# Queries, keys and values of a two-layer attention kernel: earlier requests, second buffers, merged transfers

## The chip, the cores and the metric

The kernel runs on one core of a Trainium2 chip. The metric is the device time of one execution in microseconds (us). Beside the plain runs there is one execution that was taken with the hardware profiler. All times of stages and instructions below come from that one.

## The reference

The program is a small diffusion backbone with two layers over 1024 latent tokens, with a prefix of 256 context tokens, width 1024, in fp32. The even layer (here "layer 0") has two groups of attention heads: A is global attention with 8 query heads on 2 key/value heads, and B is attention in a band of 128 tokens to either side, with a learned sink. The odd layer ("layer 1") has a convolution branch and attention D over a 2-D neighbourhood, 8 heads with a bias table. Cut to what matters here:

```python
def even_mixer(h_lat, h_ctx, w_in, w_out, ...):
    aq, ak, av, ag, bq, bk, bv, bg = project(h_lat)      # and the same of h_ctx
    aq, ak, bq, bk = (apply_rope(t, cos, sin) for t in (aq, ak, bq, bk))
    ka = concat([c_ak, ak], axis=1); va = concat([c_av, av], axis=1)
    oa = lax.map(lambda qb: gqa_attend(qb, ka, va), qa_blk)           # blocks of 128 queries
    ob = lax.map(b_block, (arange(n_blk), qb_blk))                    # context + band, bias, sink
    y = concat([oa * silu(ag), ob * silu(bg)], -1) @ w_out

def odd_mixer(...):
    oc = conformer_conv(cv, cgl, cg, ...)
    od = lax.map(d_row, (arange(rows), q_rows))   # softmax(q k^T * scale + bias) v, per head
    y = concat([oc, od * silu(dg)], -1) @ w_out

def reference(...):
    for i in range(2):
        h = rms_norm(x, norm_g[i]) * (1 + sc) + sh      # sc, sh, g = split(silu(c) @ mod_w[i] + mod_b[i])
        x = x + g * mixer(h)
    return rms_norm(x_lat, final_g)
```

## The kernel before

**Arithmetic.** Every fp32 operand of a large product is split into a high part (rounded) and a low part, and a product is three matmuls: high x high, high x low, low x high (`mm3`, L317 to L319; `split`, L297 and L300). In attention the scores need two matmuls of a tile (L444 and L448) because high and low parts of a 64-wide head lie above each other in 128 rows: `QH` holds the high part of the queries twice, `QL` the low part and some rows for the maximum; `KA` holds the high part of the keys in rows 0 to 63 and the low part in rows 64 to 127, and `KB` holds the high part once more.

**Way through DRAM.** Projections write queries, keys, values and gates to DRAM tensors (`Qd`, `Kd`, `Vd`, `Gs` in layer 0; `QD`, `KD`, `VD`, `GD` in layer 1), and the attention reads them back in another layout. In layer 0 `proj_qkv` makes them for a unit `u` (one key/value head with its four query heads), and `qk_tail` transposes one block of 128 tokens and writes its `Q` and `K` (L808, L809).

**Attention.** `attn_gen` walks over groups. In layer 0 a group is one block of 128 queries of a unit with 2, 4, 5 or 10 key tiles, ten groups for each of four units (order `ORDER`, `QORD`); in layer 1 a group is one head and one half of the latent tokens, with 7 tiles. For each tile it issues the two score matmuls into a bank `st`, the exponential on ScalarE (L456), the split into `ph` and `pl`, and three tiles later (`look`) the three products with the values into `ov` (L407 to L409). Before a group can begin, its preparation (`attn_prep`) has to be through: it requests `QH` and `QL` (`load_q`), multiplies queries and keys for the row maximum (`maxes`, banks `mx`: L548, L560, L568 in layer 0, L1245, L1253 in layer 1), and writes the maximum into rows of `QL` (L386). The preparation of group gi + 2 is a generator that is advanced while group gi runs: `g.step` steps for each tile, with what is left drained at the group's last tile. After the request it makes four empty steps before the first product.

**Buffers and loads.** In layer 0 `KA` has two buffers, `KB` and the values `V` one each. `load_ka` reads the whole of a unit's keys, in two halves, when the queries of its first group are requested; `load_kb` and the load of `V` follow when the first group begins. In layer 1 `load_head` reads the keys of the next head (L357, L358) and copies them to `KB` on ScalarE (L359); the queries come in three transfers (L1205 to L1207). All these are issued by the SyncE queue, in order. At the start the tiles of `mod_w` use the same buffers (`mw_tile`).

**Order.** `weave` interleaves the steps of `attn_gen` with filling work: the projections of the next unit (`fill0`), the output projections, in layer 1 `d_proj` and `out1_part`. A scheduler then orders the instructions of each engine by priority and by a modelled time. On the chip each engine runs its own list in order. Layer 0's attention runs from about 110 to 900 us, layer 1's from about 1110 to 1550 us.

The lines of the profile are lines of this kernel; the parts that the change touches:

Of the kernel before, what the change touches and what calls it, by code (L numbers as in the profile page):

```python
# [18 lines left out]
P = 128  # L19
# [12 lines left out]
BSO = (0, 256, 608, 1120, 1440)  # L32
BMO = (0, 320, 320, 760)
LOOK0, LOOK1 = 3, 3
AHEAD = 3
BMB = 2
CWB = 12
# [51 lines left out]
def tile_kernel(ctx: ExitStack, tc: tile.TileContext, a, out):  # L89
# [72 lines left out]
    @contextmanager  # L162
# [189 lines left out]
        GP.memset(KB[64:68, :].bitcast(F32), 1.0)  # L352
        Ks.append((KA, KB))

    def load_k(k, kh, kl):
        KA, KB = Ks[k % len(Ks)]
        SY.dma_start(KA[0:64, :].bitcast(F32), kh)  # L357
        SY.dma_start(KA[64:128, :].bitcast(F32), kl)  # L358
        SC.copy(KB[0:64, :], KA[0:64, :].bitcast(F32))  # L359

    def attn_prep(pool, g):
        QH = pool.tile([P, 512], F32R, tag="QH", name=nm("QH"), bufs=3)
        QL = pool.tile([P, 512], F32R, tag="QL", name=nm("QL"), bufs=3)
        g.QH, g.QL = QH, QL
        g.load_q(QH, QL)
        for _ in range(4):
            yield
        mp = pool.tile([P, 4, 4], F32, tag="mp", name=nm("mp"), bufs=2)
        if g.sink is not None:
            sk1, sk8 = g.sink  # L370
            SC.copy(mp[:, :, g.nmp], sk8)
# [12 lines left out]
        tr2 = bank("tr", nm("trn"))  # L384
        PE.transpose(tr2[0:nr, 0:P], nmt[:, 0:nr].bitcast(F32), ident)
        VE.tensor_tensor(QL[64 : 64 + nr, :].rearrange("p (h q) -> p h q", h=4),  # L386
                         tr2[0:nr, None, 0:P].broadcast_to([nr, 4, P]),
                         bd[0:nr, :, None].broadcast_to([nr, 4, P]), op=ALU.mult)

    def attn_gen(pool, groups, vshare, look, nexts=None):  # L390
# [30 lines left out]
                g.finish(g.ov, rb)  # L421

        for p in preps[:2]:
            for n_, _ in enumerate(p):
                if n_ % 2:
                    yield
        for gi, g in enumerate(groups):
            ids = [gi + 2] if gi + 2 < len(groups) else []
            if nexts is not None and gi in nexts:
                ids = nexts[gi]  # L430
            g.next = chain.from_iterable(preps[k] for k in ids)
            g.step = -(-18 * len(ids) // len(g.tiles))
        for g, t in items[:AHEAD]:
            g.ahead(t)
        for x, (g, t) in enumerate(items):
            if x + AHEAD < len(items):
                items[x + AHEAD][0].ahead(items[x + AHEAD][1])
            if t == 0:
                g.start()
            k, q0, n, extra = g.tiles[t]  # L440
            KA, KB = g.k()
            st = bank("st", nm("st"))
# [16 lines left out]
            pend.append((g, t, ph, pl))  # L459
            if t == len(g.tiles) // 2:  # L460
                g.gate()
            for _ in range(g.step // 2):
                next(g.next, None)
            yield
            if len(pend) > look:
                flush()
            for _ in range(g.step - g.step // 2):
                next(g.next, None)
            if t == len(g.tiles) - 1:
                for _ in g.next:  # L470
                    pass
            yield
        while pend:
            flush()
# [39 lines left out]
    KAs, KBs = [None] * 4, [None] * 4  # L514

    def load_ka(u):
        KAs[u] = a0.tile([P, NTOK], F32R, tag="KA", name=nm("KAt"), bufs=2)
        SY.dma_start(KAs[u][0:64, :].bitcast(F32), Kd[u][:, 0, :])
        SY.dma_start(KAs[u][64:128, :].bitcast(F32), Kd[u][:, 1, :])

    def load_kb(u):
        KB = KBs[0]
        SY.dma_start(KB[0:64, :].bitcast(F32), Kd[u][:, 0, :])

    def group0(u, qb):
        isb = u >= 2

        first = qb == QORD[0]
# [13 lines left out]
        def maxes(QH, mp):  # L542
# [12 lines left out]
            for hd in range(4):  # L555
# [7 lines left out]
                else:  # L563
# [30 lines left out]
        def finish(ov, rb):  # L594
# [9 lines left out]
            else:  # L604
# [5 lines left out]
        g = Group(load_q=load_q, start=(lambda: load_kb(u)) if first else (lambda: None), bias=False, ahead=lambda t: None, gate=gate, v=lambda k: Vs[0][:, k, :], load_v=(lambda: SY.dma_start(Vs[0][:, :, 0:128].bitcast(F32), Vd[u])) if first else None, maxes=maxes, nmp=1 if qb < 2 else (2 if isb else 3),  # L610
                  sink=(sink[:, hs : hs + 4], sink8[:, hs : hs + 4]) if isb else None, skm=lambda: sk, k=lambda: (KAs[u], KBs[0]),
                  tiles=[(k, 0, 512, x) for k, x in kt], den=den, finish=finish)
        g.prep = attn_prep(kvp, g)
        return g
# [4 lines left out]
    with ExitStack() as p0x:  # L619
# [181 lines left out]
        def qk_tail(u, j, pc):  # L801

            tr = bank("tr", nm("trk"))
            for i in range(3):
                PE.transpose(tr[:, i * P : (i + 1) * P], pc[:, i * P : (i + 1) * P], ident)
            qs = ap.tile([P, 2, 384], F32R, tag="qs", name=nm("qs"), bufs=2)
            split(tr[:, 0:384], qs[:, 0, :], qs[:, 1, :], "s", "v")
            SY.dma_start(Qd[u][j].rearrange("p a b t -> p a (b t)"), qs[:, :, 0:256].bitcast(F32))  # L808
            mark[0] = SY.dma_start(Kd[u][:, :, j * P : (j + 1) * P], qs[0:64, :, 256:384].bitcast(F32))  # L809

        def mod_steps():
            for part in (2,):
# [14 lines left out]

        def fill0(k, w=None):
            yield from proj_qkv(ORDER[k], w)
            yield from proj_gate(ORDER[k], gblocks(k)[0])  # L830

        for _ in fill0(0, w0):
# [1 line left out]
        solo[0] = False  # L834
        while hold[0]:
            next(mods)
        v_tiles(a0, 10)
        KBs[0] = a0.tile([P, NTOK], F32R, tag="KB", name="KBt")
        GP.memset(KBs[0][64:68, :].bitcast(F32), 1.0)
# [121 lines left out]
    with ExitStack() as l1x:  # L961
# [229 lines left out]
        v_tiles(dpool, 7, 2)  # L1191
        od = [None, None]

        def load_head(hd):
            i, e = divmod(hd, 2)
            ds = slice(e * 64, (e + 1) * 64)
            load_k(hd, KD[i][ds, 0, :], KD[i][ds, 1, :])

        def group1(gi, hd, hf):
            i, e = divmod(hd, 2)  # L1200
# [30 lines left out]
            def start():  # L1231
                if hf == 0 and hd < 7:
                    load_head(hd + 1)
                for j, k, n in ((0, 0, 2), (2, 2 + 5 * hf, 5)):
                    SY.dma_start(Vs[gi % 2][:, j : j + n, 0:128].bitcast(F32), VD[i][:, k : k + n, e])

            def maxes(QH, mp):
                KA = Ks[hd % len(Ks)][0]
# [27 lines left out]
            def finish(ov, rb):  # L1266
# [6 lines left out]
                if i == 3:  # L1273
# [1 line left out]
                    return  # L1275
                SY.dma_start(O1d[ds, i, hf], y[ds])

            g = Group(load_q=load_q, maxes=maxes, nmp=2, bias=True, ahead=ahead, sink=None, tiles=tiles, den=den, finish=finish,
                      start=start, gate=gate,
                      k=lambda: Ks[hd % len(Ks)], load_v=None, v=lambda k: Vs[gi % 2][:, k if k < 2 else k - 5 * hf, :])  # L1280
            g.prep = attn_prep(kvp, g)
            return g
# [1 line left out]
        SEQ = [(hd, hf) for hd in range(6) for hf in range(2)] + [(hd, hf) for hf in range(2) for hd in (6, 7)]  # L1284
        groups1 = [group1(gi, *x) for gi, x in enumerate(SEQ)]
        load_head(0)
        x2, ocs, od3, fin = [], [], [], [0]

        def out1_alloc():
# [246 lines left out]
```

## Time and profile before

| | |
|---|---|
| median of 3 runs | 1595.51 us (1594.14 to 1599.56) |
| the profiled execution | 1597.87 us |
| its span, first to last instruction | 1596.1 us |
| TensorE busy | 1466.4 us (92%) |
| VectorE / ScalarE / GpSimd busy | 1127.4 / 757.0 / 836.3 us |
| mean granted clock of TensorE | 0.96 |
| DMA, mean over the span | 139 GB/s, 222.01 MB |

The profile's page gives, for each engine, the time in which it was busy, then the span in 40 slices, the DMA queues, the chain of work that ended last, and the costliest groups of instructions. A group's line reads: source line, engine, operation, output <- inputs, shape, count, busy time, mean duration, and the idle time of the engine ahead of it with what ended it. PE is TensorE's matmul, PEld its weight load, DVE VectorE, ACT ScalarE, POOL GpSimd, SP SyncE; a "q" behind a name is that engine's issuing side. A matmul's own duration includes its way through the array; one of 512 columns starts 0.23 us after the one before it at full clock.

### The profile page before, as it was taken

The page shows a single profiled execution, that of the slowest core. Times are in us where ns is not written, and L with a number is a line of the kernel's source. Part 1 is how long each engine was busy: PE and PEld are TensorE (multiplying, and loading weights), DVE is VectorE, ACT ScalarE, POOL GpSimd, SP SyncE. Part 2 cuts the span into 40 slices and gives each one's busy share as a digit, 9 for nine tenths or more (in the row PEclk, how much of TensorE's full clock was granted, in tenths as well). Part 3 has the DMA queues.
Part 4 walks back from the last instruction along what each step waited for, and adds up shares of the span by engine and source line. Part 5 has one row for each costly group of instructions (what it writes and reads, how often), then busy time and mean ns, then how long its engine had stood idle before and what let it go on. Part 6 is the DMA issues. An engine that isn't in the chain of part 4 may idle for free.

```text
span 1596.1 us, 22238 instructions
## 1 busy us (share of the span) xinstructions
PE 1466.4 (92%) x6984; PEld 1185.4 (74%) x6984; DVE 1127.4 (71%) x2170; ACT 757.0 (47%) x1544; POOL 836.3 (52%) x762
## 2 busy tenths in 40 slices
PE   6889989998999989989999979999999899899895
PEld 1788867787788667668887658888777678778684
DVE  4898887488857677455568776999564466776676
ACT  2721343445444655655454664443342355545473
POOL 1561454455546667756455665665442344355575
PEclk9999989999999999999999999999999899999996
DMA  8548234532452123571111121212646778898732
GB/s 316 177 146 277 79 102 128 172 98 83 142 151 66 43 69 109 176 206 45 54 40 41 56 96 43 93 58 101 205 143 199 230 207 248 247 258 247 209 97 106
DMA packets 198654, 222.01 MB, mean 139 GB/s; under 512 B 19004, under 2 KB 154888, under 8 KB 198536
## 3 DMA queue, kind: packets, MB, share of 16 engines
q1 hardware_dynamic: 191872, 209.02, 42.9%
q10 hardware_dynamic: 6664, 11.57, 2.4%
q8 instruction: 55, 0.90, 0.2%
q14 instruction: 63, 0.52, 0.1%
HBM read 160.49 MB, written 60.03 MB: 138 GB/s over the span
## 4 chain that ended last, share of the span: by engine, by line
PE 64%; DVE 13%; DMA 12%; issue 4%; POOL 3%; ACT 2%; SPq 1%; DVEq 0%; POOLq 0%; ACTq 0%
PE p L317 6%; PE p L318 6%; PE p L319 6%; PE ov L409 4%; PE ov L407 4%; PE po L317 3%; PE ov L408 3%; PE po L318 3%; PE po L319 3%; PE st L448 3%; PE st L444 3%; PE pq L318 2%; PE pq L317 2%; PE pq L319 2%; PE pg L317 2%
## 5 line engine op out<-in xcount | busy, mean ns | idle before, releaser
L300 POOL TENSOR_TENSOR pl<-pf,ph 128x512 fp32r<-128x512 f32 (+4 forms) x321 | 394.1, 1239 | 283.4 <-ACT ph L297 226.3
L300 POOL TENSOR_TENSOR wl<-wr,wh 128x256 fp32r<-128x256 f32 (+2 forms) x256 | 199.6, 795 | 231.6 <-ACT wh L297 187.0
L456 ACT ACTIVATE pf<-st 128x512 f32<-128x512 f32 x284 | 166.3, 597 | 171.2 <-PE st L448 127.6
L297 ACT CAST ph<-pf 128x512 fp32r<-128x512 f32 (+4 forms) x364 | 209.1, 588 | 36.1 <-PE ov L408 20.8
L317 PE MATMUL p<-hh,wh 128*128 128x512 f32 x448 | 181.2, 406 | 6.1 <-DVE spq L1087 3.0
L297 ACT CAST wh<-wr 128x256 fp32r<-128x256 f32 (+2 forms) x264 | 102.7, 404 | 166.5 <-DMA wr<-in_ev_qkv_dram 40.7
L318 PE MATMUL p<-hl,wh 128*128 128x512 f32 x448 | 180.9, 405 | 0.0
L319 PE MATMUL p<-hh,wl 128*128 128x512 f32 x448 | 176.4, 402 | 0.0
L407 PE MATMUL ov<-ph,Vt 128*128 128x512 f32 (+4 forms) x364 | 142.5, 392 | 9.7 <-DVE y L598 6.4
L409 PE MATMUL ov<-pl,Vt 128*128 128x512 f32 (+4 forms) x364 | 142.9, 393 | 5.4 <-POOL pl L300 5.3
L444 PE MATMUL st<-QH,KAt 128*128 128x512 f32 (+4 forms) x364 | 141.9, 391 | 4.5 <-ACT pf L456 3.8
L408 PE MATMUL ov<-ph,Vt 128*64 128x512 f32 (+4 forms) x364 | 140.0, 385 | 0.0
L448 PE MATMUL st<-QL,KBt 68*128 68x512 f32 (+4 forms) x364 | 138.4, 389 | 0.7 <-DVE QL L386 0.7
L1027 DVE SCALAR_TENSOR_TENSOR cps<-U,taps,cps 128x512 f32<-128x512 f32 x184 | 125.2, 749 | 0.4
L561 DVE TENSOR_REDUCE mp<-mx 128x1 f32<-128x512 f32 x128 | 86.0, 683 | 48.9 <-PE mx L560 48.3
L220 DVE SCALAR_TENSOR_TENSOR macc<-mw,csil,macc 128x512 f32<-128x512 f32 x107 | 94.4, 902 | 21.6 <-DMA mw<-in_mod_w_dram 19.5
L317 PEld LDWEIGHTS p<-hh,wh 128*128 128x128 f32 x448 | 86.2, 192 | 29.1 <-issue 3.6
L319 PEld LDWEIGHTS p<-hh,wl 128*128 128x128 f32 x448 | 86.3, 193 | 20.8 <-issue 0.5
L318 PEld LDWEIGHTS p<-hl,wh 128*128 128x128 f32 x448 | 86.0, 192 | 18.9
L409 PEld LDWEIGHTS ov<-pl,Vt 128*128 128x128 f32 x364 | 70.5, 194 | 29.6 <-POOL pl L300 9.0
L407 PEld LDWEIGHTS ov<-ph,Vt 128*128 128x128 f32 x364 | 70.7, 194 | 26.1 <-issue 7.7
L319 PE MATMUL pq<-wh,hl 128*128 128x384 f32 x256 | 87.9, 345 | 0.7 <-DVE hl L311 0.7
(276 smaller groups left out, 3529.0 us busy)
## 6 DMA issues: line engine op xcount, KB each, us to landing
mw<-in_mod_w_dram SPq DMA_DIRECT2D x34, 512.0 KB, 5.5
Q<-qs SPq DMA_DIRECT2D x40, 256.0 KB, 2.7
QH<-Q SPq DMA_DIRECT2D x80, 128.0 KB, 2.8
wr<-in_od_d_dram SPq DMA_DIRECT2D x64, 128.0 KB, 2.6
mw<-in_mod_w_dram SPq DMA_DIRECT2D x28, 256.0 KB, 3.1
wr<-in_ev_qkv_dram SPq DMA_DIRECT2D x32, 192.0 KB, 3.6
KAt<-KD SPq DMA_DIRECT2D x16, 384.0 KB, 6.5
wr<-in_od_wo_dram SPq DMA_DIRECT2D x48, 128.0 KB, 3.2
```

The costliest lines, as they stand in the source:

```text
L297: SC.copy(hi, src)
L300: (GP if leng == "g" else VE).tensor_tensor(lo, src, hi.bitcast(F32), op=ALU.subtract)
L317: PE.matmul(o, lh, rh, start=first, stop=False)
L318: PE.matmul(o, lh, rl, start=False, stop=False)
L319: PE.matmul(o, ll, rh, start=False, stop=last)
L407: PE.matmul(o, V[:, 64:192], ph[:, :n], start=(t == 0), stop=False)
L408: PE.matmul(g.ov[0:64, q0 : q0 + n], V[:, 0:64], ph[:, :n], start=False, stop=False)
L409: PE.matmul(o, V[:, 64:192], pl[:, :n], start=False, stop=(last and g.sink is None))
L444: sts.append(PE.matmul(st[:, :n], KA[:, cs], g.QH[:, q0 : q0 + n], start=True, stop=False))
L448: PE.matmul(st[:, :n], KB[0:68, cs], g.QL[0:68, q0 : q0 + n], start=False, stop=True)
L456: SC.activation(pf[:, :n], st[:, :n], AF.Exp, scale=1.0 if g.bias else SCALE)
L1027: VE.scalar_tensor_tensor(pc, uc, w, pc, op0=ALU.mult, op1=ALU.add)
```

## The change

- Preparation in `attn_gen`: the request for the queries is issued when group gi begins (`next(preps[k])`), and the steps after it, the first products among them, may run from 3 tiles later on in layer 0 and 4 in layer 1 (`LEAD`). From then on `prepare` makes a fixed number of steps for each tile (`rate`: 2 or 3 for each open preparation) in place of `g.step` and the drain at the group's end.
- Layer 0's `KB` and `V` have two buffers (`kv_tiles`), so the `mod_w` tiles of the start have them too. Keys and values of the next unit are read in three pieces (`PIECES`: blocks 0 to 1, 2 to 5, 6 to 9), each as soon as its last block has been written by `qk_tail`. `KB` is filled by a copy on ScalarE (`copy_k`) in the last tile of the last group but one of the unit before; the first unit's is read from DRAM.
- Transfers: `Kd` is laid out as it is needed, high above low, and one transfer of 128 rows reads a piece. `Qd` is laid out so that a head pair's row is contiguous; two transfers write a block in place of one. `QH` is filled by one transfer that reads its source twice, in place of two, in both layers; layer 1's `KA` is read by one transfer in place of two, and its copy to `KB` moves to the last tile of a group.
- `fill0` drains the waiting `qk_tail`s ahead of the gate projection (`NFILL` counts these steps).

```diff
-NFILL = (39, 39, 36)
+LEAD = (3, 4)
+NFILL = (43, 43, 40)
...
             w = a0.tile([P, 1920 if t == "V" else NTOK], F32, tag={"A": "KA", "B": "KB", "V": "V"}[t], name=nm("mw"),
-                        bufs=2 if t == "A" else 1)
+                        bufs=2)
...
-    def load_k(k, kh, kl):
+    def load_k(k, ks):
         KA, KB = Ks[k % len(Ks)]
-        SY.dma_start(KA[0:64, :].bitcast(F32), kh)
-        SY.dma_start(KA[64:128, :].bitcast(F32), kl)
-        SC.copy(KB[0:64, :], KA[0:64, :].bitcast(F32))
+        SY.dma_start(KA.bitcast(F32), ks.rearrange("d s k -> s d k"))
+        return KA, KB
...
         g.load_q(QH, QL)
-        for _ in range(4):
-            yield
+        yield
...
+        work = []
+        def prepare(x, n):
+            while n and work and work[0][0] <= x:
+                if next(work[0][1], work) is work:
+                    work.pop(0)
+                else:
+                    n -= 1
...
             if t == 0:
                 g.start()
+                while any(p is g.prep for _, p in work):
+                    prepare(len(items), 1)
+                for k in g.ids:
+                    next(preps[k])
+                    work.append((x + LEAD[layer[0]], preps[k]))
+            rate = g.rate * max(len(work), 1)
...
-            for _ in range(g.step // 2):
-                next(g.next, None)
+            if t == len(g.tiles) - 1:
+                g.last()
+            prepare(x, rate // 2)
             yield
             if len(pend) > look:
                 flush()
-            for _ in range(g.step - g.step // 2):
-                next(g.next, None)
-            if t == len(g.tiles) - 1:
-                for _ in g.next:
-                    pass
+            prepare(x, rate - rate // 2)
             yield
...
-    Qd = [[dram(f"Q{u}_{j}", [P, 2, 2, P]) for j in range(10)] for u in range(4)]
-    Kd = [dram(f"K{u}", [64, 2, NTOK]) for u in range(4)]
+    Qd = [[dram(f"Q{u}_{j}", [64, 2, 2, 2 * P]) for j in range(10)] for u in range(4)]
+    Kd = [dram(f"K{u}", [P, NTOK]) for u in range(4)]
...
+    PIECES = {1: (0, 2), 5: (2, 6), 9: (6, 10)}
+    def load_kv(u, j0, j1):
+        ts = slice(j0 * P, j1 * P)
+        SY.dma_start(KAs[u][:, ts].bitcast(F32), Kd[u][:, ts])
+        SY.dma_start(V0s[u][:, j0:j1, 0:128].bitcast(F32), Vd[u][:, j0:j1])
+    def copy_k(KA, KB):
+        SC.copy(KB[0:64, :], KA[0:64, :].bitcast(F32))
...
         def load_q(QH, QL):
-            if first:
-                load_ka(u)
-            src = Qd[u][qb].rearrange("(e d) s a t -> d s e (a t)", e=2)
-            for dst, s in ((QH[0:64, :], 0), (QH[64:128, :], 0), (QL[0:64, :], 1)):
-                SY.dma_start(dst.bitcast(F32).rearrange("d (e c) -> d e c", e=2), src[:, s])
+            src = Qd[u][qb].rearrange("d s e c -> d s (e c)")
+            SY.dma_start(QH.bitcast(F32), src[:, 0][None].broadcast_to([2, 64, 512]))
+            SY.dma_start(QL[0:64, :].bitcast(F32), src[:, 1])
...
+        def last():
+            if qb == QORD[-2] and u != ORDER[-1]:
+                v = ORDER[ORDER.index(u) + 1]
+                copy_k(KAs[v], KBs[v])
...
             def load_q(QH, QL):                                   # layer 1
-                SY.dma_start(QH[0:64, :].bitcast(F32), QD[i][ds, 0, hf])
-                SY.dma_start(QH[64:128, :].bitcast(F32), QD[i][ds, 0, hf])
+                SY.dma_start(QH.bitcast(F32), QD[i][ds, 0, hf][None].broadcast_to([2, 64, 512]))
```

More of the change, by code (lines that the diff above doesn't have):

```diff
@@ L423, in attn_gen @@
         for p in preps[:2]:
+            next(p)
+            yield
+        for _ in range(2):
+            yield
+        for p in preps[:2]:
             for n_, _ in enumerate(p):
@@ L426, in attn_gen @@
                     yield
+        work = []
[5 more added lines that the diff above has]
+                    n -= 1
         for gi, g in enumerate(groups):
-            ids = [gi + 2] if gi + 2 < len(groups) else []
+            g.ids = [gi + 2] if gi + 2 < len(groups) else []
             if nexts is not None and gi in nexts:
-                ids = nexts[gi]
-            g.next = chain.from_iterable(preps[k] for k in ids)
-            g.step = -(-18 * len(ids) // len(g.tiles))
+                g.ids = nexts[gi]
         for g, t in items[:AHEAD]:
@@ L807, in qk_tail @@
             split(tr[:, 0:384], qs[:, 0, :], qs[:, 1, :], "s", "v")
-            SY.dma_start(Qd[u][j].rearrange("p a b t -> p a (b t)"), qs[:, :, 0:256].bitcast(F32))
-            mark[0] = SY.dma_start(Kd[u][:, :, j * P : (j + 1) * P], qs[0:64, :, 256:384].bitcast(F32))
+            for e in range(2):
+                SY.dma_start(Qd[u][j][:, :, e], qs[e * 64 : (e + 1) * 64, :, 0:256].bitcast(F32))
+            mark[0] = SY.dma_start(Kd[u].rearrange("(s d) t -> d s t", s=2)[:, :, j * P : (j + 1) * P],
+                                   qs[0:64, :, 256:384].bitcast(F32))
+            if j == 0 and not solo[0]:
+                kv_tiles(u)
+            if j in PIECES and not solo[0]:
+                load_kv(u, *PIECES[j])
         def mod_steps():
@@ L829, in fill0 @@
             yield from proj_qkv(ORDER[k], w)
+            while tails and k:
+                qk_tail(*tails.pop(0))
+                yield
             yield from proj_gate(ORDER[k], gblocks(k)[0])
@@ L836, in tile_kernel @@
             next(mods)
-        v_tiles(a0, 10)
-        KBs[0] = a0.tile([P, NTOK], F32R, tag="KB", name="KBt")
-        GP.memset(KBs[0][64:68, :].bitcast(F32), 1.0)
+        assert not tails
+        kv_tiles(ORDER[0])
+        for j in PIECES:
+            load_kv(ORDER[0], *PIECES[j])
+        SY.dma_start(KBs[ORDER[0]][0:64, :].bitcast(F32), Kd[ORDER[0]][0:64])
         main = attn_gen(a0, [group0(u, qb) for u in ORDER for qb in QORD], VS0, LOOK0)
@@ L1192, in tile_kernel @@
         od = [None, None]
+        heads = {}
         def load_head(hd):
@@ L1235, in start, with last @@
                     SY.dma_start(Vs[gi % 2][:, j : j + n, 0:128].bitcast(F32), VD[i][:, k : k + n, e])
+            def last():
+                if hf == 0 and hd < 7:
+                    copy_k(*heads[hd + 1])
             def maxes(QH, mp):
@@ L1276, in finish @@
                 SY.dma_start(O1d[ds, i, hf], y[ds])
-            g = Group(load_q=load_q, maxes=maxes, nmp=2, bias=True, ahead=ahead, sink=None, tiles=tiles, den=den, finish=finish,
-                      start=start, gate=gate,
+            g = Group(load_q=load_q, maxes=maxes, nmp=2, bias=True, rate=3, ahead=ahead, sink=None, tiles=tiles, den=den, finish=finish,
+                      start=start, gate=gate, last=last,
                       k=lambda: Ks[hd % len(Ks)], load_v=None, v=lambda k: Vs[gi % 2][:, k if k < 2 else k - 5 * hf, :])
@@ L1286, in tile_kernel @@
         load_head(0)
+        copy_k(*heads[0])
         x2, ocs, od3, fin = [], [], [], [0]
```

24 lines of the change are left out of this document (13 added, 11 removed).

## The prediction

> **What bounds the kernel now.** I read the page first, then busy time by stage, then TensorE's waits within the two attention stages, and last the chain of waits around the longest of them.
>
> ```profile
> span 1596.1 us, 22238 instructions
> PE 1466.4 (92%) x6984; PEld 1185.4 (74%) x6984; DVE 1127.4 (71%) x2170; ACT 757.0 (47%) x1544; POOL 836.3 (52%) x762
> PE 64%; DVE 13%; DMA 12%; issue 4%; POOL 3%; ACT 2%; SPq 1%; DVEq 0%; POOLq 0%; ACTq 0%
> ```
>
> TensorE is the bound, and the change takes no matmul away: both programs hold the same 6,812. So it can only change TensorE's idle time and its clock. Busy time by stage (columns: TensorE, its weight loads, VectorE, ScalarE, GpSimd, granted clock, busy share of the 16 DMA engines, GB/s):
>
> ```profile
> 200.00:720.00 520.00, 477.25 (x2283) 385.71 (x2284) 361.66 (x735) 258.67 (x526) 300.92 (x242) 0.96 0.40 119
> 720.00:885.00 165.00, 164.95 (x787) 132.83 (x786) 106.10 (x189) 85.04 (x158) 91.02 (x79) 1.00 0.14 44
> 1230.00:1530.00 300.00, 277.39 (x1351) 224.96 (x1350) 190.51 (x461) 149.42 (x319) 139.00 (x151) 0.97 0.81 229
> ```
>
> Layer 0's attention idles 520 - 477.3 = 42.7 us, then not at all from 720 to 885. Layer 1's idles 22.6 us, with the DMA engines busy 81% of the time. TensorE's waits for queries and keys (us in total, times, longest; the first two rows are layer 0's, the others layer 1's):
>
> ```profile
> PE mx L548 <- DMA QH<-Q: 8.2, 5, 2.7
> PE mx L548 <- DMA KAt<-K: 5.9, 1, 5.9
> PE mx L1245 <- DMA QH<-QD: 6.2, 4, 2.4
> PE mx L1245 <- DMA KAt<-KD: 4.8, 2, 3.0
> ```
>
> Together 25.1 us: all that earlier requests can take away directly. The longest, in the chain of waits (start, duration):
>
> ```profile
> 671.28 2.86 DMA K<-qs
> 674.21 0.49 SPq L518
> 674.75 8.75 DMA KAt<-K
> 683.64 1.20 PE mx L548 x4
> 684.84 0.43 PE ov L409
> ...
> 688.23 0.23 PE mx L560
> ```
>
> The last unit's keys are written, land, and are only then read whole, and TensorE waits. It pays twice: up to about 687 a matmul takes 0.43 us, afterwards 0.23.
>
> **Part 1: keys ahead of time.** I laid the two instruction orders side by side and counted the matmul work (0.23 us for 512 columns) between what frees a buffer and the first product that needs the load. The last piece of the keys now has 33, 14 and 37 us at the three changes of unit, where the whole load had 10, 8 and 4. The wait of 5.9 us goes, and with it some 4 us of slow clock (683 to 687), in which half the time was lost: 2 us. At an earlier change of unit the queries queue behind the keys:
>
> ```profile
> 307.60 5.36 DMA QH<-Q
> 312.95 0.25 issue
> 313.20 1.19 PE mx L548 x4
> 315.03 0.32 PE pq L319
> 316.95 0.43 PE ov L409
> ```
>
> TensorE's gap there was 2.7 us, by the longest in the wait row, and slow matmuls follow until about 318: 3 us more. Sum of part 1: 5.9 + 2 + 2.7 + 3 = 14 us saved, all on the path. The Trainium skill (TensorE: Matmul & The Clock Gate, Part 1) lets the clock fall after an idle window of about 3.4 us. By that rule the second stall would cost no clock and the part would be 11 us; here 2.7 us of idling was enough.
>
> `KB` is now a ScalarE copy. Layer 1 has such copies already:
>
> ```profile
> L359 ACT CAST KBt<-KAt x8: 1462/1472/1481, 1238.4 to 1480.8; 64x1536 fp32r<-64x1536 f32 x8
>   DMA KAt<-KD: 21.5, 6
> ```
>
> Three more of 1280 columns cost about 1.2 us each on an engine that is 47% busy, hidden by the exponentials already queued; without that cover 3.7 us. In layer 1 the second row counts what ScalarE idles in front of them, and exponentials queue behind it; in the new order they still stand close behind their load. `V` shows no TensorE wait before, so its second buffer gains nothing directly. Its first piece can wait at the head of SyncE's queue for the unit before last, with stores and requests behind it: 0 to 3 us, twice.
>
> **Part 2: merged transfers.** This decides the sign. Counts and sizes from the DMA issues (KB each, median us from issue to landing), and the packets:
>
> ```profile
> QH<-Q SPq DMA_DIRECT2D x80, 128.0 KB, 2.8
> KAt<-KD SPq DMA_DIRECT2D x16, 384.0 KB, 6.5
> cst<-in_k_sk_dram SPq DMA_DIRECT2D x1, 38.0 KB
> k_bd<-in_k_bd_dram ACTq DMA_DIRECT2D x1, 0.2 KB
> DMA packets 198654, 222.01 MB, mean 139 GB/s; under 512 B 19004, under 2 KB 154888, under 8 KB 198536
> q1 hardware_dynamic: 191872, 209.02, 42.9%
> ```
>
> The new `QH` load is one transfer of 256 KB whose source, as the built program has it, counts 2 (step 0) x 64 x 512; layer 1's new `KA` load is 768 KB and counts 2 x 64 x 1536. Every transfer of the old program leads with 12, 64, 76, 128 or more rows, so the trace shows none like these. It does show what the leading count does. The program issues 1,116 transfers, and its tables of short rows make 1,164 data packets under 512 B. That leaves 19,004 - 1,164 = 17,840 small packets: 16 for each transfer would be 17,856, and 16 are missing. The two transfers whose rows 16 doesn't divide, 76 rows (`k_sk`) and 12 rows (`k_bd`), explain exactly that if they ran on 4 and 12 engines, each engine reporting once. So the number of engines divides the leading count, and with a leading 2 it would be two of sixteen. The Trainium skill (DMA: Bandwidth & Descriptors, Why a DMA increments its semaphore by 16 and not by 1, and Rules for kernel authors) says this of both sides of a transfer, and names a leading zero-stride broadcast as the case that confines it.
>
> Price. The q1 row gives 209.02 MB / (0.429 x 16 x 1596.1 us) = 19.1 GB/s for a busy engine. Spread over 16, a `QH` half is 8 KB an engine, 0.4 us, so 2.8 - 0.4 = 2.4 us are fixed. On two engines `QH` takes 2.4 + 131 KB / 19.1 = 9.3 us, `KA` 2.4 + 393 / 19.1 = 23 us, and a `QH` right behind it 30 us; everything else behind them waits for its share on those two engines. The other bound is 2.8 us and 6.5 us as now, less one issue of 0.6 us. I take two engines: the count of packets is the nearest row.
>
> Against that stands the lead. Four empty steps before, three or four tiles now, yet in the orders themselves the matmul work between freeing `QH` and its first product is hardly changed: layer 0, without the first three groups, median 7.7 us before and after. The scheduler had already placed the products where it thought the queries ready. 22 of 37 groups have under 9.3 us, and their shortfalls add up to 83 us. In layer 1 a new head's keys have 6 to 12.6 us against 30; seven heads (the first at 23 us, its queries being there) are short by 142 us, and second halves by some 25 us.
>
> Not all of that is lost: other waits pass in the meantime, and layer 0's stage is 520 us for some 445 us of matmul work (its 2,283 matmuls at 0.23 us for 512 columns), so a lead lasts longer than its work. I take 60% of 83 = 50 us, and 70% of 167 = 117 us. Slow clock after some 15 longer stalls: the one above cost 2 us; half of such stalls stand where a shorter one slows the clock today, so I take 1 us each: 15 us. Off goes what is waited today and lies within these: 8.2 + 6.2 + 4.8 = 19 us. Part 2: 50 + 117 + 15 - 19 = 163 us lost.
>
> A check by load: in the last stage row the DMA engines are busy 0.81 x 300 = 243 us. Two of them get, less what they now have of it, 8 x 20.6 + 16 x 6.9 = 275 us more, minus about 30. Near 490 us of work on two engines in a 300 us stage is +190 us if all of it must pass there; with less contention, less. 117 us lies within that.
>
> **Part 3: the rest.** A block of queries is stored by two transfers (40 more), loads save 40 + 16 + 8, and pieces add some: SyncE has 1,061 in place of 1,076, about 0.6 us each, not on the path. The new pace of the preparation keeps every instruction and moves them; about as many products follow closely on what they need. -5 to +5 us, taken as 0. What the DMA engines moved in each of 40 slices:
>
> ```profile
> GB/s 316 177 146 277 79 102 128 172 98 83 142 151 66 43 69 109 176 206 45 54 40 41 56 96 43 93 58 101 205 143 199 230 207 248 247 258 247 209 97 106
> ```
>
> At the start second buffers let `mod_w` tiles be requested earlier; one tile of 512 KB now stands ahead of `x` on a queue that moves 316 GB/s there (1.7 us), against fewer waits for buffers: 0.
>
> **The sum.** The profiled execution took 1597.9 us, 1.8 beyond its span and 2.4 above the median of 1595.5. 1597.9 - 14 + 163 = 1747 us, less the 2.4: 1744 us.
>
> **Rivals.**
> *All sixteen engines (0.13; faster).* If the repeated source is spread over all engines after all, `QH` lands in 2.8 us or less with one issue fewer, the count of short leads falls to almost none, and part 1 stays: -14, some -3 for queries in layer 1, +6 for pieces at the head of SyncE's queue (twice 3 us, the upper bound): 1595.5 - 11 = 1584.5, say 1585 us. For it: a merged transfer is no bigger than two halves. The Trainium skill's Rules for kernel authors (same page) advise one transfer of 128 partitions in place of two halves. Point of decision: the landing of `QH` in layer 0, under 3.5 or over 7 us.
> *Leads cover more (0.25; slower).* With two engines, but the waits overlapping better: a stalled TensorE also holds back the loads behind, so the two engines run empty and faster than 19.1 GB/s. Layer 0 then loses 20, layer 1 65 us, clock 5, and 14 saved: 1595.5 + 76 = 1672 us.
> *SyncE blocked (0.04; no change).* No slow transfers, but the piece of `V` and pieces of keys, waiting for their writes to land, hold up weights by what part 1 saves: 1596 us.
>
> **How the numbers follow.** Forecast 0.58, the rivals 0.25, 0.13, 0.04. With full shortfalls and 25 us for the clock the first is 83 + 167 + 25 - 19 - 14 = +242: 1838 us; the second at its lower end, with layer 1 at 45: +50, 1645 us. The range 1645 to 1838 us leaves out the faster rival and the unchanged one, 0.17 together. About 0.3% is what a measurement of this kernel can tell from no change. Faster 0.13, same 0.04, slower 0.83.
>
> **What would show it.** Right: TensorE's wait for `KAt<-K` in layer 0 is gone; `QH<-Q` lands after about 9 us and `KAt<-KD` after over 20; TensorE's waits of first products (`mx`) for them grow to tens of us in layer 0 and over 70 in layer 1; packets under 512 B fall short of 16 a transfer by 14 for each merged one (64 x 14 = 896); the granted clock falls in layer 1. Wrong: `QH` lands in 3 us and the shares of the stages stay as they are, or TensorE's waits stay below 30 us although the loads are long.

## The result, and the profile after

The changed kernel takes 1829.24 us (median of 4 runs, 1826.23 to 1830.09) against 1594.83 before: ratio 1.1456, 95% interval 1.1419 to 1.1493. The page of the profiled execution (1829.3 us), its span, busy times and packets:

```profile
span 1827.6 us, 22268 instructions
PE 1511.2 (83%) x6984; PEld 1220.4 (67%) x6984; DVE 1129.8 (62%) x2170; ACT 765.3 (42%) x1547; POOL 832.9 (46%) x764
PE 53%; DMA 28%; DVE 10%; issue 3%; POOL 2%; SPq 2%; ACT 2%; DVEq 0%; ACTq 0%; POOLq 0%
DMA packets 190671, 221.03 MB, mean 121 GB/s; under 512 B 17868, under 2 KB 138904, under 8 KB 190552
```

The span grew by 231.5 us. TensorE's busy time grew by 44.8 us for the same matmuls, which is clock; its idle time grew from 129.7 to 316.4 us, by 186.7. In the chain that ended last, DMA went from 12 to 28%. Stages of the changed kernel (columns as before: TensorE, weight loads, VectorE, ScalarE, GpSimd, clock, DMA share, GB/s):

```profile
200.00:900.00 700.00, 615.97 (x2859) 498.45 (x2857) 435.87 (x866) 323.42 (x643) 363.76 (x299) 0.93 0.31 95
1300.00:1750.00 450.00, 295.80 (x1336) 239.86 (x1335) 189.54 (x449) 147.24 (x309) 130.91 (x145) 0.82 0.51 155
```

Layer 1's attention needs 450 us for about as many matmuls (1,336) as it did in 300 (1,351). The engines of the DMA are busy 51% of it instead of 81%, and still TensorE waits for them: two loaded engines among sixteen would look like that in a mean. TensorE's waits for queries, keys and split weights, and one wait of ScalarE (total, times, longest):

```profile
PE mx L1291 <- DMA QH<-QD: 99.7, 10, 18.1
PE mx L573 <- DMA QH<-Q: 53.1, 18, 5.9
PE mx L1291 <- DMA KAt<-KD: 27.2, 2, 15.1
PE p L318 <- ACT wh L298: 22.4, 2, 13.3
ACT KBt L552 <- DMA KAt<-KD: 122.3, 8, 17.0
```

The first three rows are 180.0 us in place of 25.1. The row `KAt<-K` of 5.9 us is gone. The landings, from the chain of waits (start, duration; two of layer 0, then layer 1):

```profile
507.52 7.52 DMA QH<-Q
682.73 8.48 DMA QH<-Q
...
1195.82 10.24 DMA KD<-spk
1329.47 25.81 DMA KAt<-KD
1355.35 4.74 DMA wr<-in_od_d_dram
1380.96 9.05 DMA QH<-QD
1401.53 23.25 DMA QH<-QD
1439.82 8.37 DMA QH<-QD
1460.04 23.78 DMA QH<-QD
```

Layer 1 alternates: a half whose queries come alone waits for 8.4 to 10.8 us of landing, a half whose queries stand behind the next head's keys for 23 to 25.

The fourth row of the waits is ScalarE's split of the weights, late twice. TensorE stood still for 13.3 us up to 1360 us, where the weights were requested only when the keys had landed, and for 9.1 us up to 1207 us, where ScalarE itself had waited 12.5 us for a store of `KD` that was issued right behind merged query loads. The last row is ScalarE alone. Its queue holds the copy to `KB` ahead of later exponentials and splits, and it idled 122.3 us in front of the eight copies of layer 1, against 25.2 us with the merges undone (after_split, below).

### The profile page after: what moved, and what is told of

The parts are those of the page before. It is cut to its first block, busy times and chain, and to the rows that moved or that the text cites. A ratio compares the mean times of both kernels' runs of the same rounds, so it can differ in the third digit from the quotient of the medians.

```text
span 1827.6 us, 22268 instructions
## 1 busy us (share of the span) xinstructions
PE 1511.2 (83%) x6984; PEld 1220.4 (67%) x6984; DVE 1129.8 (62%) x2170; ACT 765.3 (42%) x1547; POOL 832.9 (46%) x764
## 2 busy tenths in 40 slices
DMA packets 190671, 221.03 MB, mean 121 GB/s; under 512 B 17868, under 2 KB 138904, under 8 KB 190552
## 4 chain that ended last, share of the span: by engine, by line
PE 53%; DMA 28%; DVE 10%; issue 3%; POOL 2%; SPq 2%; ACT 2%; DVEq 0%; ACTq 0%; POOLq 0%
DMA QH<-QD 9%; DMA QH<-Q 8%; PE p L318 5%; PE p L319 5%; PE p L320 5%; PE po L318 3%; PE po L320 3%; PE po L319 3%; PE st L462 3%; PE st L466 3%; PE ov L408 3%; PE ov L406 2%; PE ov L407 2%; PE pq L318 2%; PE pq L320 2%
## 5 line engine op out<-in xcount | busy, mean ns | idle before, releaser
L318 PE MATMUL p<-hh,wh 128*128 128x512 f32 x448 | 183.2, 410 | 26.7 <-ACT wh L298 22.4
L462 PE MATMUL st<-QH,KAt 128*128 128x512 f32 (+4 forms) x364 | 148.3, 409 | 16.8 <-ACT pf L474 16.1
L408 PE MATMUL ov<-pl,Vt 128*128 128x512 f32 (+4 forms) x364 | 146.8, 403 | 3.7 <-POOL pl L301 2.8
L466 PE MATMUL st<-QL,KBt 68*128 68x512 f32 (+4 forms) x364 | 143.6, 405 | 4.1 <-DVE QL L385 4.1
L1291 PE MATMUL mx<-KAt,QH 128*128 128x256 f32 x64 | 18.6, 370 | 130.8 <-DMA QH<-QD 99.7
L221 DVE SCALAR_TENSOR_TENSOR macc<-mw,csil,macc 128x512 f32<-128x512 f32 x107 | 93.8, 895 | 32.6 <-DMA mw<-in_mod_w_dram 31.8
L1291 PEld LDWEIGHTS mx<-KAt,QH 128*128 128x128 f32 x64 | 13.6, 238 | 137.0 <-issue 74.7
L575 DVE TENSOR_REDUCE mp<-mx 128x2 f32<-128x512 f32 x80 | 53.7, 688 | 82.9 <-PE mx L573 82.5
```

The costliest lines, as they stand in the source:

```text
L318: PE.matmul(o, lh, rh, start=first, stop=False)
L408: PE.matmul(o, V[:, 64:192], pl[:, :n], start=False, stop=(last and g.sink is None))
L462: sts.append(PE.matmul(st[:, :n], KA[:, cs], g.QH[:, q0 : q0 + n], start=True, stop=False))
L466: PE.matmul(st[:, :n], KB[0:68, cs], g.QL[0:68, q0 : q0 + n], start=False, stop=True)
```

## The experiments

Theory: a transfer whose source leads with a count of 2 runs on two of the sixteen DMA engines, and all of the loss comes from the three merged transfers. Rivals: the new pace of the preparation, loads that wait in SyncE's queue, or a source that is slow because it is read twice over.

| run | time, us | ratio to before (95%) |
|---|---|---|
| after_split | 1587.4 | 0.9913 (0.9881 to 0.9944) |
| before_merged | 1841.8 | 1.1508 (1.1466 to 1.1549) |
| l0_q_merged, one run | 1678.2 | |
| l1_k_merged, one run | 1691.6 | |
| l1_q_merged, one run | 1647.4 | |
| repeat_16_4, one run | 1606.7 | |
| kd_rows | 1583.7 | 0.9906 (0.9874 to 0.9937) |
| l0_lead4, one run | 1642.2 | |
| split_lead4 | 1578.6 | 0.9866 (0.9839 to 0.9892) |
| old_prep | 1579.7 | 0.9883 (0.9855 to 0.9910) |
| late_keys | 1590.5 | 0.9938 (0.9917 to 0.9958) |
| one_piece | 1587.0 | 0.9914 (0.9890 to 0.9939) |

The kernel before took 1598 to 1601 us (medians) beside these runs, a little more than beside the first.

**All merges undone (after_split).**

```diff
-            SY.dma_start(QH.bitcast(F32), src[:, 0][None].broadcast_to([2, 64, 512]))
+            for h in range(2):
+                SY.dma_start(QH[h * 64 : (h + 1) * 64, :].bitcast(F32), src[:, 0])
...
-        SY.dma_start(KA.bitcast(F32), ks.rearrange("d s k -> s d k"))
+        for h in range(2):
+            SY.dma_start(KA[h * 64 : (h + 1) * 64, :].bitcast(F32), ks[:, h])
...
-                SY.dma_start(QH.bitcast(F32), QD[i][ds, 0, hf][None].broadcast_to([2, 64, 512]))
+                for h in range(2):
+                    SY.dma_start(QH[h * 64 : (h + 1) * 64, :].bitcast(F32), QD[i][ds, 0, hf])
```

> The changed kernel with nothing undone but the merges: QH of both layers by two transfers of 64 rows, KA of layer 1 by two. Theory (a source that leads with a count of 2 runs on two DMA engines): landings of QH fall back to about 2.8 us in layer 0 and 4 to 6 us in layer 1, of KA to 6 to 7 us, TensorE's waits for QH<-QD and KAt<-KD from 127 us to about 10, small packets under 512 B back to 16 a transfer (56 + 8 transfers more, 64 x 16 + 896 = 1,920 more), time 1575 to 1600 us, by the prediction's part 1 about 1582. Rival (the new pace of the preparation, or loads waiting in SyncE's queue, cost the time): over 1680 us, the waits for QH stay.

Its page, its waits and its DMA issues:

```profile
span 1594.3 us, 22328 instructions
PE 1469.8 (92%) x6984; PEld 1183.9 (74%) x6984; DVE 1130.4 (71%) x2170; ACT 766.5 (48%) x1547; POOL 836.5 (52%) x764
PE st L463 <- ACT pf L475: 17.7, 16, 3.1
PE mx L1294 <- DMA QH<-QD: 5.4, 4, 2.3
DMA packets 192590, 221.03 MB, mean 139 GB/s; under 512 B 19788, under 2 KB 140824, under 8 KB 192472
QH<-Q SPq DMA_DIRECT2D x80, 128.0 KB, 2.8
KAt<-KD SPq DMA_DIRECT2D x16, 384.0 KB, 6.4
```

The loss is gone, and a gain of 0.9% is left. The small packets are exactly the 19,788 foretold. So the whole of the loss stands in three lines of the diff.

**Only the merges (before_merged).** The same three merged transfers, and the layout and stores of `Qd` that they need, in the kernel before.

```diff
-            for dst, s in ((QH[0:64, :], 0), (QH[64:128, :], 0), (QL[0:64, :], 1)):
-                SY.dma_start(dst.bitcast(F32).rearrange("d (e c) -> d e c", e=2), src[:, s])
+            SY.dma_start(QH.bitcast(F32), src[:, 0][None].broadcast_to([2, 64, 512]))
+            SY.dma_start(QL[0:64, :].bitcast(F32), src[:, 1])
...
-        SY.dma_start(KA[0:64, :].bitcast(F32), kh)
-        SY.dma_start(KA[64:128, :].bitcast(F32), kl)
+        SY.dma_start(KA.bitcast(F32), ks.rearrange("d s k -> s d k"))
...
```

> The kernel before with nothing but the three merges (and the new layout of Qd in DRAM with its second store, without which the merged load of layer 0 can't be written). Theory (two engines): QH lands in 8 to 9 us alone and about 24 behind KA, KA in 19; the requests come no earlier than they did, so the loss is that of the changed kernel or somewhat more: 1800 to 1860 us. Rival (pace of the preparation or queue order): under 1620 us.

Its two longest waits for queries:

```profile
PE mx L1244 <- DMA QH<-QD: 83.1, 8, 18.3
PE mx L547 <- DMA QH<-Q: 48.9, 16, 5.5
```

1841.8 us: the merges alone, without any of the rest, cost all of it. The changed kernel waits no less for its queries (99.7 and 53.1 us): its earlier requests took nothing off these two rows. Its ratio of 1.1456 and this one's of 1.1508 have intervals that overlap.

**One merge at a time (l0_q_merged, l1_k_merged, l1_q_merged).** after_split with one of the three merged lines put back.

> The changed kernel with QH of layer 1 and KA of layer 1 split again; only layer 0's QH stays merged (40 transfers, small packets 40 x 14 = 560 short). Theory: layer 0 keeps its loss, some 70 us above before between 200 and 960 us, layer 1 is as before: 1640 to 1670 us. Rival (losses of layer 0 come from the preparation): time as of after_split within 10 us, or layer 0 stays slow there as well.

> The changed kernel with QH split in both layers; only layer 1's KA stays merged (8 transfers of 768 KB). Theory: KA lands in about 17 us, and the split QH behind it no earlier, since its share on the two busy engines waits for them; most of layer 1's 150 us stays: 1680 to 1730 us. Rival (it is the merged QH that costs in layer 1, KA only delays its own first product): under 1640 us.

> The changed kernel with layer 0's QH and layer 1's KA split; only layer 1's QH stays merged (16 transfers). Theory (what hurts in layer 1 is the queue behind KA on the two engines): QH alone lands in 8 to 9 us against leads of 6 to 12, a loss of 10 to 35 us: 1597 to 1622 us. Rival (costs of the parts simply add: after_split 1587, layer 0's QH +91, KA +104, the whole about 1832): the rest of 50 us falls to it, 1635 us or more.

Busy time and wait of l0_q_merged, then waits and landings of l1_k_merged, then of l1_q_merged:

```profile
PE 1492.7 (89%) x6984; PEld 1204.9 (72%) x6984; DVE 1130.3 (67%) x2170; ACT 764.7 (46%) x1547; POOL 833.7 (50%) x764
PE mx L574 <- DMA QH<-Q: 53.1, 17, 5.9
```

```profile
PE mx L1293 <- DMA QH<-QD: 59.4, 7, 13.9
PE p L318 <- ACT wh L298: 14.8, 2, 14.5
...
1359.89 18.36 DMA QH<-QD
1412.05 22.60 DMA KAt<-KD
1462.09 19.23 DMA QH<-QD
1493.82 4.22 DMA QH<-QD
```

```profile
PE mx L1293 <- DMA QH<-QD: 38.9, 7, 8.9
...
1353.55 9.51 DMA QH<-QD
1376.62 13.47 DMA QH<-QD
```

Over after_split's 1587 us they cost 91, 104 and 60 us; together 255, where the changed kernel lies 242 above it (1829.2 to 1587.4, from two sessions). They add up to within 13 us, from single runs. In l1_k_merged the queries are spread over all sixteen engines again, and behind the keys they land after 18 to 19 us all the same, against 4.2 us where no keys are ahead. That fits two loaded engines that hold back their share of the queries. Of the expectations the first fell short by 8 us (1678 against 1670 at most), and in the second the keys landed after 19 to 26 us and not 17. The third was wrong, and its rival right: merged queries alone lose 60 us and not 10 to 35. Their landing is 9 to 13 us; shares of other loads on the same two engines would explain that, but no run isolates them.

**Another count ahead (repeat_16_4).** The same size, the same number of transfers, but a source read 16 times over in layer 0 and 4 times in layer 1, so that part of the queries is not loaded:

```diff
-            SY.dma_start(QH.bitcast(F32), src[:, 0][None].broadcast_to([2, 64, 512]))
+            SY.dma_start(QH.bitcast(F32), src[0:8, 0][None].broadcast_to([16, 8, 512]))
...
-                SY.dma_start(QH.bitcast(F32), QD[i][ds, 0, hf][None].broadcast_to([2, 64, 512]))
+                SY.dma_start(QH.bitcast(F32), QD[i][e * 64 : e * 64 + 32, 0, hf][None].broadcast_to([4, 32, 512]))
```

> The changed kernel with KA of layer 1 by two transfers, and with other counts ahead in the merged QH: in layer 0 the first 8 rows of the queries' high part 16 times over, in layer 1 the first 32 rows 4 times over; sizes (256 KB) and numbers of transfers stay, the queries themselves are wrong in part. Theory (the leading count sets the number of engines): layer 0 runs on 16, QH lands in 2 to 3 us and layer 0 is as fast as in after_split; layer 1 on 4, 64 KB an engine, QH lands in 5 to 6 us (half of the 9 us on two engines, less the fixed part); packets under 512 B are 16 short for none of the 40 and 12 for each of the 16: 19,788 - 56 x 16 - 192 = 18,700; time 1585 to 1610 us. Rival (a source that is read several times over with step 0 is slow, whatever its count): layer 0 keeps its waits of 53 us, QH lands in 8 us or more, 1670 us or more.

Its packets, layer 0's issues, layer 1's wait, and the shortest and the longest landing there that the chain of waits holds:

```profile
DMA packets 191503, 221.04 MB, mean 138 GB/s; under 512 B 18700, under 2 KB 139736, under 8 KB 191384
QH<-Q SPq DMA_DIRECT2D x40, 256.0 KB, 3.4
PE mx L1292 <- DMA QH<-QD: 18.5, 6, 5.4
...
1380.05 6.16 DMA QH<-QD
...
1400.58 11.77 DMA QH<-QD
```

In layer 0, 256 KB land in 7.4 to 8.5 us with 2 ahead and in 3.4 us with 16. In layer 1 the 4 ahead show less in the landings than was expected: 6.2 to 11.8 us in place of 5 to 6, where 2 ahead had 9.0 to 13.5 (l1_q_merged). They do show in TensorE's wait for these queries: 38.9 us with 2, 18.5 with 4, and 5.4 with the two halves on all sixteen engines (after_split). 18,700 small packets, as worked out: 4 and 16 reports for a transfer. Reading a source 16 times over is thus not slow in itself; the count ahead decides. The keys say the same from the other side, since their source has no step of 0 and was slow too.

**A merged transfer with 128 rows ahead (kd_rows).** `KD` holds a head's high part above its low part, and `KA` is read by one transfer of 768 KB again.

```diff
-    KD = [dram(f"KD{i}", [P, 2, 12 * P]) for i in range(4)]
+    KD = [dram(f"KD{i}", [2, P, 12 * P]) for i in range(4)]
...
+        SY.dma_start(KA.bitcast(F32), ks)
...
```

> after_split (all merges undone) with KD laid out in DRAM so that a head's high part stands above its low part, 128 rows in a row, and KA of layer 1 read by one transfer of 768 KB again; 20 more stores. Theory (only the leading count of 2 hurts, not the merging): KA lands in 5 to 7 us as its halves did, layer 1 as in after_split, 1580 to 1595 us. Rival (a transfer of 768 KB blocks what is behind it): KA lands in 10 us or more, over 1610 us.

```profile
KAt<-KD SPq DMA_DIRECT2D x8, 768.0 KB, 5.8
```

5.8 us for what took 19 to 26 with a leading 2: here merging is harmless where the rows stand in one run.

**A longer lead (l0_lead4, split_lead4).** A fourth `QH` and `QL` in layer 0, requests one group earlier within a unit, and two `pc` buffers in place of three; once with layer 0's `QH` merged, once with it split.

```diff
-PCB = 3
+PCB = 2
...
+        x4 = layer[0] == 0 and turn[0] % 4 == 0
-        QH = pool.tile([P, 512], F32R, tag="QH", name=nm("QH"), bufs=3)
+        QH = pool.tile([P, 512], F32R, tag="QX" if x4 else "QH", name=nm("QH"), bufs=1 if x4 else 3)
...
-                for k in g.ids:
-                    next(preps[k])
+                for k in range(len(asked), min(gi + 4, len(groups))) if layer[0] == 0 else g.ids:
+                    if layer[0] or k < gi + 3 or k // 10 == gi // 10:
+                        next(preps[k])
+                        asked.append(k)
...
```

> l0_q_merged (only layer 0's QH merged, 1678 us) with a fourth buffer of QH and QL in layer 0, and each group's queries but those of the first two or three groups of a unit requested one group earlier (pc has two buffers instead of three to make room). Theory (the 8 us landing costs only what the lead doesn't cover): the lead grows by a whole group, over 10 us, TensorE's wait for QH<-Q falls from 53 us to under 15, time 1595 to 1625 us. Rival (two engines are overloaded, what waits is everything behind them): the wait falls by less than half, time over 1650 us.

> The control of l0_lead4: the same fourth buffer, earlier requests and two pc buffers, with QH split everywhere (all 16 engines). Theory (l0_lead4's 1642 us hold little of the slow landing any more, the rest is the price of the other edits, above all of the pc buffer): 1605 to 1635 us, ratio 1.005 to 1.02. Rival (the longer lead hides the wait on QH itself but the two engines still cost 50 us elsewhere): 1580 to 1595 us, as after_split.

The wait of l0_lead4, and busy time of both:

```profile
PE mx L583 <- DMA QH<-Q: 11.6, 8, 2.5
PE 1483.7 (90%) x6984; PEld 1193.5 (73%) x6984; DVE 1119.3 (68%) x2170; ACT 766.3 (47%) x1547; POOL 832.6 (51%) x764
```

```profile
PE 1463.2 (93%) x6984; PEld 1182.2 (75%) x6984; DVE 1130.5 (72%) x2170; ACT 766.5 (49%) x1547; POOL 835.5 (53%) x764
```

The lead took the wait itself from 53.1 to 11.6 us, as the first theory had it, but only 36 us came off (1678 to 1642), not the 53 or more that it named. The theory of the control fell, and its rival came true: the other edits are no price. With them and split loads the kernel is as fast as any here, 1578.6 us, and 1.3% faster than before. So 64 us of a slow landing stay when the wait for it is mostly hidden: 20.5 us of clock (busy time), 11 of what is left of the wait, and the rest in waits of a few microseconds, most of them for ScalarE and VectorE, no one row over 8 more than in the control. What drives those stays open.

**What the gain comes from (old_prep, late_keys, one_piece).** after_split with the preparation of before, without the draining of `qk_tail`s, and with keys and values read in one piece:

```diff
-            prepare(x, rate // 2)
+            for _ in range(g.step // 2):
+                next(g.next, None)
...
```

```diff
-NFILL = (43, 43, 40)
+NFILL = (39, 39, 36)
...
-            while tails and k:
-                qk_tail(*tails.pop(0))
-                yield
```

```diff
-    PIECES = {1: (0, 2), 5: (2, 6), 9: (6, 10)}
+    PIECES = {9: (0, 10)}
```

> after_split (all merges undone) with the preparation of before: four empty steps after the request, steps by g.step, drained at the group's last tile; no LEAD. Keys and values keep their buffers and pieces. Theory (the prediction's parts 1 and 3: the keys bring the gain, the new pace and the earlier request for queries nothing, -5 to +5 us): ratio 0.988 to 0.995. Rival (the queries' earlier request brings the gain): 0.997 to 1.003.

> after_split without the draining of the waiting qk_tails ahead of the gate projection (NFILL back to 39, 39, 36): the last block of a unit's keys is written and read later. Theory (the gain comes from the lead of the keys' last piece, 33, 14 and 37 us): a wait for KAt<-K of 2 to 8 us is back, ratio 0.993 to 1.000. Rival (second buffers and pieces are enough, the draining brings nothing): 0.988 to 0.993, no wait for KAt<-K.

> after_split with each unit's keys and values read by one transfer each after the last block, not in three pieces. Theory (what counts is that the request stands long before the first product, not how much of it is left to load): ratio as after_split, 0.988 to 0.995, no wait for KAt<-K over 1 us. Rival (the pieces shorten what is waited for): a wait for KAt<-K of 3 us or more, 0.996 or more.

No gain of the new preparation shows: without it the kernel is 1.2% faster than before, and its interval overlaps that of after_split. Nor does one of the pieces: one load of the whole has 0.9914 against 0.9913. Without the draining 0.6% are left, with an interval that overlaps after_split's too. The wait for `KAt<-K` that the theory of that run foretold did not come back, so how much the draining brings stays open. What remains in all three are the second buffers, requests for keys that no longer stand behind the first queries of the unit, and the new layout of `Qd` and `Kd`. No run takes these apart, so which of them makes the gain is not shown.

## Why the prediction came true, and where it was off

The sign, the mechanism and the range held: 1829 against 1744 forecast and 1645 to 1838 stated. That it still lies within the range is in part luck. The upper end took every shortfall in full, 250 us, and 25 us of slow clock; measured are 180 us of these waits, 44.8 us of clock and 31.8 us of waits that stood in no bound. Three slips in the working are small. The 2.7 us of a late query load come off twice, in part 1 and within the 8.2 of part 2; the lower end of the second rival is 20 + 45 + 5 - 14 = 56 us by its own terms and not 50, so 1652 us; and the 6,812 matmuls stand as 6,984 on the page, before and after. By its steps, on the profiled executions (forecast 1747, measured 1829, so 82 short):

- **The number of engines: right.** 1,101 transfers with 16 reports each, less the 16 of `k_sk` and `k_bd`, and 1,164 data packets make 18,764; 64 merged transfers with 14 fewer make 17,868, the page's number to the packet. The rule of the Trainium skill (DMA: Bandwidth & Descriptors, Rules for kernel authors) that a small outermost count confines a transfer is thus borne out here by the packets for 2, 4 and 16. Its advice on the same list, to use one transfer of 128 partitions for two halves, holds in kd_rows (5.8 us against 6.4 for the halves) and fails in all three merges whose source leads with 2; the faster rival that rested on it would have given about what after_split measured, 1587 against 1585.
- **Landings: right in kind, those of the queries too long.** 9.3 us were forecast for the queries alone, and layer 0 shows 7.4 to 8.5; for queries behind keys 30, and 23 to 25 came; for the keys 23, and the runs with merged keys show 19 to 26. By the landings of layer 0 an engine moves 131 KB in some 8.0 - 2.4 us, an estimate of 23 GB/s in place of the 19.1 that was taken as the mean of all its work.
- **The discount: wrong, and it made up for that.** 60 and 70% of the shortfalls were taken, 50 and 117 us; the waits are 53.1 and 126.9 us. With the true landings the shortfalls shrink by some 22 x 1.2 us in layer 0 and 7 x 6 in layer 1, to about 57 and 125 us, an estimate, and nearly all of that is lost. Less the waits of before (19 us in part 2, 5.9 and 2.7 in part 1) the forecast for these waits was +139 us, and the trace shows 154.9.
- **The clock: the step that failed most.** 15 stalls at 1 us, less 5 saved, against 44.8 us. There are 30 waits for queries and keys in place of 12, many short ones of layer 0 among them; 44.8 us is 2.5 us for each of the 18 that are new, if all of it is put down to them. What a short one does, from the timeline of TensorE (start, duration; in brackets the idle time before):

```profile
1444.95 0.39 PE L406 MATMUL ov<-ph,Vt 128*128 128x512 f32 x1
1445.19 0.39 PE L407 MATMUL ov<-ph,Vt 128*64 128x512 f32 x1
...
1448.24 0.79 PE L1291 MATMUL mx<-KAt,QH 128*128 128x256 f32 x2 [2.34 <-DMA QH<-QD]
...
1449.63 0.63 PE L319 MATMUL p<-hl,wh 128*128 128x512 f32 x1
1450.05 0.63 PE L320 MATMUL p<-hh,wl 128*128 128x512 f32 x1
1450.48 0.63 PE L318 MATMUL p<-hh,wh 128*128 128x512 f32 x1
...
1451.69 0.39 PE L318 MATMUL p<-hh,wh 128*128 128x512 f32 x1
1451.92 0.39 PE L319 MATMUL p<-hl,wh 128*128 128x512 f32 x1
```

  Starts are 0.24 us apart ahead of the 2.34 us of idling, 0.42 behind it and 0.23 later. The same in two stretches of 3.41 us (columns as in the stages above, the clock third from the end):

```profile
1444.76:1448.17 3.41, 1.14 (x7) 0.66 (x5) 0.95 (x2) 1.32 (x3) 0.73 (x1) 1.00 0.55 158
1448.17:1451.58 3.41, 3.34 (x9) 2.82 (x10) 2.41 (x6) 0.86 (x2) 0.00 (x0) 0.50 0.33 83
```

  TensorE was busy for 1.14 us of the first stretch, and the second ran at half the clock throughout. So a stall of 2.3 us cost up to 1.7 us, half of 3.41, and the 1 us taken for each was too little. In the trace's record of the granted clock all stretches at half speed but the last are whole multiples of 3.41 us, 23 stretches before and 45 after; by the mean clocks of 0.960 and 0.905 they sum to about 128 and 347 us, part of which TensorE idles anyway. The window of about 3.4 us in the Trainium skill (TensorE: Matmul & The Clock Gate, Part 1) agrees in its length, but it need not be idle throughout, as it is there: a third of this one was busy. The prediction was right to go by the trace.
- **What stands behind the slow loads: left out.** That "everything else behind them waits for its share" was written and priced at nothing. The other 31.8 us of idle time lie there in the main, the weights' 22.4 us first of all (0.2 in after_split, 14.8 in l1_k_merged, 9.4 in l1_q_merged). Nor did the prediction follow ScalarE. It held the copies to `KB` to be cheap because they stand close behind their load, but with loads of 19 to 26 us ScalarE idled 122.3 us in front of the eight copies of layer 1, with exponentials and splits of weights behind. How much of layer 1's loss goes through ScalarE no run separates.
- **Part 1: the size right, perhaps by luck, its working not shown.** -14 us forecast, 1 - 0.9913 of 1600 us = 14 measured, 9 to 19 by the interval. The wait for `KAt<-K` is gone as foretold. But the profiled run of after_split is the slowest of its five (1596.1 us), with waits for `pf` up from 3.8 to 17.7 us, so its rows can't bear out the four terms one by one.
- **Part 3, the pace at 0: right** within what old_prep can tell.

## What to carry to other kernels

Before two transfers are merged into one, write down the counts of the source's access pattern: here a leading 2 put the whole on two of sixteen DMA engines, and loads issued after it came late too, whatever their own spread (18 to 19 us in place of 4.2). Lay the source out so that 128 rows stand in one run, or leave two transfers of 64 rows; here that turned 15% slower into 1% faster. When stalls are priced, price the slow clock behind each one, the loads that queue behind the slow one, and the other engines that wait for it, in the same sum.

## What the runs showed of the hardware

The packets under 512 B serve as a count of engines. With 16 reports for a transfer whose leading count 16 divides, and 2, 4 or 12 for the others, the sum came out exact to the packet in every kernel where it was worked out (17,868, 18,700 and 19,788 above); in the traces these reports are 4 bytes long. A 256 KB load of layer 0 takes about 8 us with a leading 2 and 3.4 with a leading 16. A stretch of 3.41 us in which TensorE was busy for a third was followed by one at half the clock. And a load whose wait is mostly hidden can still cost: with the wait down to 11.6 us, 64 us stayed.
